# A hybrid encoder layer on one core: more attention rows turned by TensorE, turns a unit ahead, one more buffer for projection tiles

## The chip, the cores and the metric

The kernel runs on one core of a Trainium2 chip. The metric is the device time of one execution in microseconds (us); the median over runs is compared. Beside the runs there is one profiled execution, whose records make up the trace. TensorE (PE) multiplies matrices; VectorE (DVE), ScalarE (ACT) and GpSimd (POOL) work element by element; SyncE (SP) issues most DMA transfers. Each engine carries out its own instructions in order and waits for others by semaphores.

## The reference, cut to what matters

One encoder layer over 1024 tokens with 1024 features: a norm, one combined projection, two groups of attention heads beside each other, an output projection, and a gated MLP. The change lies in the attention.

```
proj = hn @ w_in;  qa, ka, va, qb, kb, vb = split(proj)
# group A: 8 query heads on 2 key heads, window |i - j| <= 128, a sink logit per head
p = softmax([q k / 8 within the window, sink]);  o_a = p v
# group B: 8 heads over a 16 x 64 grid of tokens, 8 x 16 neighbourhood, relative bias
p = softmax(q k / 8 + bias);                     o_b = p v
h = x + concat(rmsnorm(o_a), rmsnorm(o_b)) @ w_out
h = h + (silu(conv3(hn @ w_gate)) * (hn @ w_up)) @ w_down;  out = rmsnorm(h)
```

## The kernel before

**Splits.** All large products are made in three passes: a high and a low half of each operand, high by high, high by low and low by high (lines 156 to 158 for the projection). Every weight tile is loaded in two parts of 128x512 (`fetch_w`), copied to its high half by ScalarE (L148, `whi`), and its low half is a subtraction (L149, `wlo`) on DVE, or on POOL once the attention is well under way.

**Projection as filler.** The projection's columns are 18 jobs (`Project`), and then 8 jobs of the output projection for group A (`OutA`). Each job is 16 blocks of three matmuls of 128x512 into PSUM tiles `pj`; DVE moves a finished `pj` to a tile `t` of the pool "temps" (L224, L228), which has three buffers. The first three jobs are done ahead; the rest are spread as filler between the pieces of attention, by numbers per unit (`RATES`).

**Start.** Jobs 0 to 2 give the first key, value and queries of group A. Their rotation folds rows by DMA (`f<-t`), turns them on DVE (L242 to L244) and sends them back by DMA (`t<-f`, L246). Then come the stacks of high and low halves: keys (`split_first_k`, L271 to L274), queries (`split_first`, L264 and L265). The value tile is split to 16-bit halves `vhl`, a tile in "temps", and turned by a transposing DMA (L329, `v<-vhl`) that SyncE issues like the others. Loading of the second weight part of the third filler job is put behind the stacks.

**Attention.** There are 16 units of group A (a block of 128 queries, four heads each) and 32 of group B (a pair of query blocks, four units per head). A row is one query block of one head against up to three neighbouring key blocks. Its steps: TensorE makes the scores `s` (L378); DVE adds mask or bias, takes the extremum and writes `p` (L408); ScalarE exponentiates with the sum (L412); DVE takes the reciprocal (L413). Then the probabilities must be turned, keys to partitions, as two 16-bit halves in a tile `turned`, by one of three paths:

- D: ScalarE scales and copies the high half (L426), DVE makes the low half (L427), a transposing DMA turns both (L428).
- P: POOL scales (L416), ScalarE copies the high half (L422), POOL makes the low half (L423), a transposing DMA turns both.
- T: POOL scales (L416), TensorE transposes `p` block by block into the PSUM tile `pt` (L434), ScalarE copies the high half (L437), DVE makes the low half (L438).

Group A's four rows go by "DPTT", group B's eight rows of a head by "DPDPDPDP". TensorE then multiplies values by the turned rows into `o` (L461 in A, L534 in B), ScalarE and DVE take `o` out (L472 and L476; L548 and L550). Beside B, group A's result is squared and normed (L185, L187, L195, L218, L772), and POOL makes the bias tiles (L492, L493).

**Order.** TensorE's order is the program's, written out by the loop over units: in unit u the value products of u, the scores of a unit two or three ahead (`LEAD`), the turns of unit u itself (`T_AT`), and filler. The other engines and the DMA queues are ordered by a scheduler. Rings set what can run ahead: six tiles `p` (`PS`), four of `turned` (`TURNED`), with some rows of both groups in spare tiles of another pool (`SPARE_A`, `SPARE_B`: in B units 1 and 3 of heads 0 to 3, unit 3 of heads 4 and 5, none in heads 6 and 7), three staging tiles (`hl`, `stage`) for the DMA paths, two PSUM tiles each of `s`, `pt`, `o` and `pj`.

Of the kernel before, what the change touches and what calls it, by code (L numbers as in the profile page):

```python
# [34 lines left out]
FILL0, FILL1 = 22, 12  # L35
RATES = [41, 49, 22, 22, 22, 22, 20, 18, 16, 14]
AHEAD = 4
TURNED, PS, HLS, SPARE_A, LOWS = 4, 6, 1, (2, 5), 1
LEAD = 3
BIAS0 = 8  # L40
T_AT = (0, 4)
PATH_A, PATH_B = "DPTT", "DPDPDPDP"
SPARE_B = [(1, 3), (1, 3), (3,), ()]
WARM = 8

# [15 lines left out]
def hybrid_layer(tc, xT, w_in, w_out, w_gate, w_up, w_down, small, sink, rpb, consts, rope, out):  # L61
    nc = tc.nc
    with ExitStack() as ctx:
# [4 lines left out]
        attention_pools = ctx.enter_context(ExitStack())  # L68
        inner = lambda name, bufs: attention_pools.enter_context(tc.tile_pool(name=name, bufs=bufs))
        wpool = inner("weights", 3)  # L70
        tpool = inner("temps", 3)
        apool = inner("att", 2)
        spool = inner("stats", 6)
        vpool = inner("values", 4)
# [3 lines left out]
        def big(name, tag, dt=F32):  # L78
            return lpool.tile([128, S], dt, name=name, tag=tag, bufs=slots[tag])
# [7 lines left out]
        f32 = lambda ap: ap.bitcast(F32)  # L87
# [57 lines left out]
        def halve_w(raw):  # L145

            hi, lo = (wpool.tile([128, 4, 128], F32R, name=n, tag=n) for n in ("whi", "wlo"))
            mark["weights"] = nc.scalar.activation(hi, raw, AF.Copy)  # L148
            mark["weights low"] = (nc.gpsimd if LOWS and mark.get("attention") else nc.vector).tensor_tensor(lo, raw, f32(hi[:, :, :]), op=ALU.subtract)  # L149
            return [(hi[:, j, :], lo[:, j, :]) for j in range(4)]  # L150

        def load_w(src):
# [144 lines left out]
            nc.sync.dma_start(f32(a[o:o + 64, :]), f32(b[e:e + 64, :]))  # L297
            return a, b

        both = []  # L300
        gains, ups = cpool.tile([128, 8], F32, name="gains"), [None] * 8

        def scaled_gain(i, up, c):
# [3 lines left out]
        def split_v(t, rows):  # L307

            n = rows.stop - rows.start
            top, down = (vpool.tile([128, 1], F32, name=x, tag=x) for x in ("top", "down"))  # L310
            up = cpool.tile([128, 1], F32, name="up", tag="up", bufs=6)
            nc.vector.tensor_reduce(top[rows], t[rows, :], axis=mybir.AxisListType.X, op=ALU.max, apply_absolute_value=True)
            nc.vector.tensor_scalar(top[rows], top[rows], TINY, None, op0=ALU.max)
            nc.vector.tensor_scalar(top[rows].bitcast(I32), top[rows].bitcast(I32), 0x7F800000, None, op0=ALU.bitwise_and)
            nc.vector.reciprocal(down[rows], top[rows])
            nc.vector.tensor_scalar(down[rows], down[rows], V_TOP, None, op0=ALU.mult)
            nc.vector.tensor_scalar(up[rows], top[rows], 1.0 / (V_TOP * P_TOP), None, op0=ALU.mult)
            if n == 64:
                nc.gpsimd.tensor_copy(up[0:64], up[rows])
            flat = tpool.tile([128, 2 * S], F16, name="vhl", tag="t", padded_shape=[128, 2 * S + 4])  # L320
            hl = flat[:, :].rearrange("p (c s w) -> p c s w", s=2, w=128)
            if n == 128 or not both:
                both.append(big("v", "op").bitcast(F16)[:, :].rearrange("p (e c s w) -> p e c s w", c=NB, s=2, w=64))
            v = both[-1] if n == 128 else both[0][:, len(va):len(va) + 1]
            src = t[rows, :].rearrange("p (c w) -> p c w", w=128)
            mark["value"] = nc.scalar.activation(hl[rows, :, 0], src, AF.Copy, scale=down[rows])
            nc.vector.scalar_tensor_tensor(hl[rows, :, 1], src, down[rows], hl[rows, :, 0], op0=ALU.mult, op1=ALU.subtract)
            for i, k in enumerate(range(rows.start, rows.stop, 64)):
                nc.sync.dma_start(v[:, i].rearrange("p c s w -> p (c s) w"), flat[k:k + 64], transpose=True)  # L329
# [167 lines left out]

        def units_grid(h):

            st = {"begun": [False, False]}  # L500
            e = 64 * (h % 2)
            me, other = slice(e, e + 64), slice(64 - e, 128 - e)

            def q_step(b):
                def go():
                    if b == 0:
                        bias_of[h] = bias_of.pop(h, None) or bias_tiles(h)
                    if b == 4 and h < 7:
                        bias_of[h + 1] = bias_tiles(h + 1)
                    x = bias_of[h]  # L510
                    if b % 2 == 0:
                        st[b // 2] = Rows(b // 2 in SPARE_B[h // 2])
                    sel = slice(2, 5, 2) if b == 0 else slice(0, 3, 2) if b == NB - 1 else slice(1, 4)
                    ps, n = scores(qb[h], kb[h], b, True)
                    st[b // 2].softmax(PATH_B[b], b % 2, ps, n, x[:, sel, :], None, int(b == 0))
                return go

            def v_step(c):
                def go():
                    if c == 0:  # L520
                        st["o"] = [bank("o", "o") for _ in range(2)]
                    for half in range(2):
                        inb = [b for b in near(c) if b // 4 == half]
                        if not inb:
                            continue
                        final = c == (4 if half == 0 else NB - 1)
                        pairs = sorted({b // 2 for b in inb})
                        for k in pairs:
                            mine = [b for b in inb if b // 2 == k]
                            dst = st["o"][half][:, (mine[0] % 4) * 128:(mine[-1] % 4 + 1) * 128]  # L530
                            runs = st[k].tile[:, :, :, :, :].rearrange("p b i s q -> p (b i) s q")
                            k0 = 3 * (mine[0] % 2) + c - mine[0] + 1
                            for s in range(2):
                                nc.tensor.matmul(dst, vb[h][:, c], runs[:, k0:k0 + 2 * len(mine) - 1:2, s], start=not st["begun"][half],  # L534
                                                 stop=final and s == 1, skip_group_check=True)
                                st["begun"][half] = True
                        if final:
                            leave(half)
                return go

            def leave(half):
                i = 4 + h // 2
                if mix[i] is None:
                    mix[i] = big("mixb", "mix")
                ot = apool.tile([128, HALF], F32, name="ot", tag="ot", bufs=1)
                w = lambda ap: ap.rearrange("p (b r c) -> p b r c", r=ROWS, c=8)
                o = st["o"][half]
# [5 lines left out]
            return [([q_step(2 * i), q_step(2 * i + 1)], [v_step(c) for c in chunks[i]], []) for i in range(4)]  # L553


        done = set()
# [100 lines left out]
        t = quarters(big("f", "mix"))  # L657
# [13 lines left out]
        raw, hi, lo = big("raw3", "mix"), big("whi3", "mix", F32R), big("wlo3", "mix", F32R)  # L671
# [29 lines left out]
        with tc.high_priority(offset=400):  # L701
            with behind("turned"):
                turn(third.m, third.t)
            with behind("value"):
                nc.scalar.activation(warm, eps, AF.Exp)

        live = {"op": 0}
        needs = lambda m: 2 if m < 6 else 3 if m % 3 else 1
# [19 lines left out]
        def rest():  # L728
            for i, job in enumerate(jobs[1:]):
# [15 lines left out]
                        aux[i, n]()  # L745
                if i == 0:
                    with behind("stack", "copied"):
                        jobs[2].load_rest()
                    with behind("weights", "weights low"):
                        make_stacks(third)  # L750
                if isinstance(job, Project):
# [37 lines left out]
        for g in range(2):  # L789
            for b in range(NB):  # L790
                q, t, w = unit_window(g, b)
# [8 lines left out]
        flat = []  # L800
# [43 lines left out]
        for u in range(len(flat)):  # L844
            q, t, need, kind, _ = flat[u]
# [690 lines left out]
```

## Time and profile before

| | |
|---|---|
| median of 3 runs (lowest, highest) | 1095.08 us (1090.98, 1095.76) |
| profiled execution, its time | 1093.65 us |
| its span, first to last instruction | 1091.9 us |
| mean granted TensorE clock | 0.986 |
| busy, share of the span: PE, DVE | 96%, 79% |
| ACT, POOL | 51%, 17% |
| DMA packets under 512 bytes | 89408 of 150157 |

The span is 1.75 us shorter than the time of the same execution. Windows of the trace are in us from the span's start. In its rows a form such as `128x384 f16<-128x384 f32 x24 | 16.9, 705 | 3.7` gives shapes and count, the time in all and the mean of one in ns, and the idle time before them with what ended it. Matmuls overlap, so their own durations add up to more than the time that passes; how far apart they start tells what one costs.

### The profile page before, as it was taken

The numbers are of one execution on the slowest core, as the hardware profiler recorded it, in microseconds if no ns is written. First come the engines' busy times: TensorE is split into PE (matmuls) and PEld (weight loads), VectorE is DVE, ScalarE is ACT, GpSimd is POOL, SyncE is SP. The second block draws the span as 40 slices with busy tenths as digits, with TensorE's granted clock in tenths as the row PEclk, the third lists the DMA queues.
The fourth block names the chain that finished last, engine by engine and source line by source line (L and its number), as shares of the span: only waits on it lengthen the run. The fifth ranks groups of instructions, "written<-read, shape, count | busy, mean of one in ns | idle before, by whom it ended". The sixth has DMA issues, their size and how long they took to land.

```text
span 1091.9 us, 14925 instructions
## 1 busy us (share of the span) xinstructions
PE 1045.9 (96%) x4950; PEld 844.8 (77%) x4950; DVE 859.5 (79%) x1671; ACT 553.7 (51%) x1047; POOL 180.5 (17%) x263
## 2 busy tenths in 40 slices
PE   9988999999888899999999999999999999999997
PEld 7766677777666687787788888888888887888887
DVE  7688888766876588899988877877887857997764
ACT  7166777666666534545434334342433545554451
POOL 2324444455554300000000000000000000000001
PEclk9989999999999899999999999999999999999998
DMA  7335464798799736314333222322322788866644
GB/s 274 74 75 128 111 127 96 149 181 157 137 148 198 166 120 230 107 36 147 146 133 118 106 106 97 116 97 105 117 88 97 238 280 280 293 225 229 207 158 154
DMA packets 150157, 165.14 MB, mean 151 GB/s; under 512 B 89408, under 2 KB 100672, under 8 KB 150080
## 3 DMA queue, kind: packets, MB, share of 16 engines
q1 hardware_dynamic: 139424, 138.43, 46.3%
q10 hardware_dynamic: 10656, 25.76, 6.3%
q8 instruction: 39, 0.64, 0.2%
q14 instruction: 38, 0.31, 0.1%
HBM read 103.58 MB, written 28.57 MB: 121 GB/s over the span
## 4 chain that ended last, share of the span: by engine, by line
PE 53%; DVE 9%; DMA 5%; issue 1%; ACT 1%; POOL 0%; DVEq 0%; SPq 0%; ACTq 0%
PE dn L932 5%; PE dn L931 5%; PE dn L933 5%; PE z L933 4%; PE z L931 4%; PE z L932 4%; PE x L931 3%; PE x L932 3%; PE x L933 3%; PE y L933 3%; PE y L931 3%; PE y L932 3%; DMA raw<-in_w_down_dram 2%; DVE wlo L921 2%; PE pj L156 2%; PE pj L157 2%
## 5 line engine op out<-in xcount | busy, mean ns | idle before, releaser
L920 ACT ACTIVATE whi<-ws 128x512 fp32r<-128x512 f32 (+1 forms) x100 | 60.2, 623 | 129.1 <-DVE ws L1037 82.5
L932 PE MATMUL dn<-xd,whi 128*128 128x512 f32 (+1 forms) x330 | 123.9, 376 | 0.8 <-DVE xd L1250 0.8
L931 PE MATMUL dn<-xd,whi 128*128 128x512 f32 (+1 forms) x330 | 124.1, 376 | 0.0
L933 PE MATMUL dn<-xd,wlo 128*128 128x512 f32 (+1 forms) x330 | 123.8, 375 | 0.0
L156 PE MATMUL pj<-xgh,whi 128*128 128x512 f32 x248 | 108.3, 437 | 6.1 <-DVE t L228 3.4
L1357 POOL TENSOR_TENSOR h<-h,wide 128x256 f32<-128x256 f32 (+1 forms) x6 | 5.4, 926 | 626.6 <-ACT wide L1353 626.6
L933 PE MATMUL z<-hg,wlo 128*128 128x512 f32 x264 | 103.1, 390 | 0.6 <-DVE wlo L921 0.6
L931 PE MATMUL z<-hg,whi 128*128 128x512 f32 x264 | 102.8, 390 | 0.0
L932 PE MATMUL z<-hg,whi 128*128 128x512 f32 x264 | 102.7, 389 | 0.0
L158 PE MATMUL pj<-xgh,wlo 128*128 128x512 f32 x248 | 99.3, 400 | 1.6 <-DVE wlo L149 1.6
L157 PE MATMUL pj<-xgl,whi 128*128 128x512 f32 x248 | 98.8, 399 | 0.0
L412 ACT ACTIVATE p<-p,nm 128x385 f32<-128x385 f32 (+3 forms) x128 | 74.5, 583 | 35.7 <-DVE nm L408 28.2
L921 DVE TENSOR_TENSOR wlo<-ws,whi 128x512 fp32r<-128x512 f32 (+1 forms) x100 | 66.6, 680 | 18.1 <-ACT whi L920 18.0
L921 DVE TENSOR_TENSOR wlo<-raw,whi 128x512 fp32r<-128x512 f32 (+1 forms) x90 | 58.7, 672 | 21.8 <-ACT whi L920 19.4
L920 ACT ACTIVATE whi<-raw 128x512 fp32r<-128x512 f32 (+1 forms) x90 | 53.8, 615 | 38.1 <-DMA raw<-in_w_down_dram 15.1
L932 PEld LDWEIGHTS dn<-xd,whi 128*128 128x128 f32 x330 | 62.1, 188 | 12.6 <-DVE xd L1250 1.5
L1249 ACT ACTIVATE xd<-xd 128x512 fp32r<-128x512 f32 x77 | 47.0, 625 | 48.0 <-DMA xd<-x 47.8
L933 PEld LDWEIGHTS dn<-xd,wlo 128*128 128x128 f32 x330 | 62.1, 188 | 11.1
L931 PEld LDWEIGHTS dn<-xd,whi 128*128 128x128 f32 x330 | 62.1, 188 | 11.1
L933 PE MATMUL y<-hg,wlo 128*128 128x512 f32 x176 | 68.7, 390 | 1.4 <-DVE wlo L921 1.4
L1250 DVE TENSOR_TENSOR xd<-xd 128x512 fp32r<-128x512 f32 x77 | 51.9, 686 | 22.1 <-ACT xd L1249 21.6
L931 PE MATMUL x<-hg,whi 128*128 128x512 f32 x176 | 68.7, 390 | 0.0
(228 smaller groups left out, 2663.7 us busy)
## 6 DMA issues: line engine op xcount, KB each, us to landing
xd<-x SPq DMA_DIRECT2D x77, 256.0 KB, 4.7
raw<-in_w_down_dram SPq DMA_DIRECT2D x64, 256.0 KB, 4.1
raw<-in_w_gate_dram SPq DMA_DIRECT2D x22, 512.0 KB, 3.3
raw<-in_w_up_dram SPq DMA_DIRECT2D x22, 512.0 KB, 3.6
x<-c ACTq DMA_DIRECT2D x22, 512.0 KB, 2.9
raw<-in_w_in_dram SPq DMA_DIRECT2D x32, 256.0 KB, 3.0
raw<-in_w_down_dram SPq DMA_DIRECT2D x32, 192.0 KB, 4.4
x<-t ACTq DMA_DIRECT2D x11, 512.0 KB, 2.7
```

The costliest lines, as they stand in the source:

```text
L156: nc.tensor.matmul(ps, w[0], x[0][:, tsl(h)], start=first, stop=False)
L157: nc.tensor.matmul(ps, w[0], x[1][:, tsl(h)], start=False, stop=False)
L158: nc.tensor.matmul(ps, w[1], x[0][:, tsl(h)], start=False, stop=last)
L412: nc.scalar.activation(p[:, 0:e], p[:, 0:e], AF.Exp, bias=nm, scale=-1.0, accum_out=sm)
L920: nc.scalar.activation(hi, src, AF.Copy)
L921: nc.vector.tensor_tensor(lo, src, f32(hi[:, :, :]), op=ALU.subtract)
L931: nc.tensor.matmul(ps, w[0], x[0], start=first and i == 0, stop=False, skip_group_check=True)
L932: nc.tensor.matmul(ps, w[0], x[1], start=False, stop=False, skip_group_check=True)
L933: nc.tensor.matmul(ps, w[1], x[0], start=False, stop=last and i == len(ws) - 1, skip_group_check=True)
L1249: nc.scalar.activation(hi, f32(lo), AF.Copy)
L1250: nc.vector.tensor_tensor(lo, f32(lo), f32(hi), op=ALU.subtract)
L1357: nc.gpsimd.tensor_tensor(x, x, copy[:, cols], op=ALU.mult)
```

## The change

- `PATH_B` is now a list by head: "PPTPPPTP" for heads 0 and 1, "TPTPTPTP" for heads 2 to 7. No row of B goes by D. Where before 32 rows of B went by D and 32 by P, there are now 36 by P and 28 by T.
- The turns are no longer made in their own unit. In unit u stand the turns of unit u + 1, at places 3 and 8 among the events of group A's units (`T_NEXT`), at 0 and 3 for group B (`T_B`); only unit 0 keeps its own.
- The rings: "temps" gets a fourth buffer, `turned` goes from 4 to 3, `p` from 6 to 5.
- Before the filler begins, `vhl` lies in a tile of the pool of operands ("op") instead of "temps", and the first transposing DMA of values is held back and issued behind the last rotated rows of jobs 0 to 2 (the mark "back").
- POOL instead of DVE makes the low half of one early weight part (the mark "early").

```diff
-TURNED, PS, HLS, SPARE_A, LOWS = 4, 6, 1, (2, 5), 1
+TURNED, PS, HLS, SPARE_A, LOWS = 3, 5, 1, (2, 5), 1
-PATH_A, PATH_B = "DPTT", "DPDPDPDP"
+PATH_A, PATH_B = "DPTT", ["PPTPPPTP"] * 2 + ["TPTPTPTP"] * 6
+T_B, T_NEXT = (0, 3), (3,8)
...
-        tpool = inner("temps", 3)
+        tpool = inner("temps", 4)
...
-            mark["weights low"] = (nc.gpsimd if LOWS and mark.get("attention") else nc.vector).tensor_tensor(lo, raw, f32(hi[:, :, :]), op=ALU.subtract)
+            mark["weights low"] = (nc.gpsimd if mark.get("attention") or mark.get("early") else nc.vector).tensor_tensor(lo, raw, f32(hi[:, :, :]), op=ALU.subtract)
...
-            flat = tpool.tile([128, 2 * S], F16, name="vhl", tag="t", padded_shape=[128, 2 * S + 4])
+            if mark.get("begun"):
+                flat = tpool.tile([128, 2 * S], F16, name="vhl", tag="t", padded_shape=[128, 2 * S + 4])
+            else:
+                flat = big("vhl", "op").bitcast(F16)
...
+            if mark.get("begun"):
+                across()
+            else:
+                postponed.append(across)
...
-                    st[b // 2].softmax(PATH_B[b], b % 2, ps, n, x[:, sel, :], None, int(b == 0))
+                    turn[b] = st[b // 2].softmax(PATH_B[h][b], b % 2, ps, n, x[:, sel, :], None, int(b == 0))
...
+            later = lambda b: lambda: turn[b]()
+            return [([q_step(2 * i), q_step(2 * i + 1)], [v_step(c) for c in chunks[i]], [later(b) for b in (2 * i, 2 * i + 1) if PATH_B[h][b] == "T"]) for i in range(4)]
...
+            with behind("back"):
+                postponed.pop()()
+        mark["begun"] = True
...
                     with behind("stack", "copied"):
+                        mark["early"] = True
                         jobs[2].load_rest()
+                        mark["early"] = False
...
-            for i, w in enumerate(flat[u][4]):
-                events.insert(T_AT[i], ("v", w))
+            if u == 0:
+                for i, w in enumerate(flat[u][4]):
+                    events.insert(T_AT[i], ("v", w))
+            if u + 1 < len(flat):
+                for i, w in enumerate(flat[u + 1][4]):
+                    events.insert((T_NEXT if u < 15 else T_B)[i], ("v", w))
```

What moves is shown at three places by the order of the built programs, where line numbers of the changed one are up to 20 higher.

SyncE's queue at the start, before: `f<-t` folds rows, `t<-f` and `t<-turns` send rotated rows back, `v<-vhl` turns the first values.

```order
L240 DMA f<-t 128x1x128 x2
L240 DMA turns<-t 128x1x128
L329 DMA_TRANSPOSE v<-vhl 128x16x64
L246 DMA t<-f 16x8x128 x4
L246 DMA t<-turns 16x8x128 x2
```

The same place now:

```order
L241 DMA f<-t 128x1x128 x2
L241 DMA turns<-t 128x1x128
L247 DMA t<-f 16x8x128 x4
L247 DMA t<-turns 16x8x128 x2
L334 DMA_TRANSPOSE v<-vhl 128x16x64
```

The transposing DMA went from before the six rows that go back to behind them.

TensorE in a unit of head 4 of group B, before: scores, filler, then values by turned rows.

```order
L378 MATMUL s<-ka,q 128x256
L378 MATMUL s<-kb,q 128x256
L156 MATMUL pj<-xgh,whi 128x512
L157 MATMUL pj<-xgl,whi 128x512
L158 MATMUL pj<-xgh,wlo 128x512
L534 LDWEIGHTS v
```

The same scores now:

```order
L388 MATMUL s<-ka,q 128x256
L388 MATMUL s<-kb,q 128x256
L157 MATMUL pj<-xgh,whi 128x512
L158 MATMUL pj<-xgl,whi 128x512
L159 MATMUL pj<-xgh,wlo 128x512
L444 MATMUL pt<-cst,p 128x128 x3
```

A turn of three blocks, for the unit after, now stands at the head of the unit, ahead of its value products.

POOL on the first rows of group B, before: L416 scales a row, L423 makes its low half, L149 is a weight's low half.

```order
L423 TENSOR_TENSOR hl<-p,hl 128x3x128
L416 TENSOR_SCALAR p<-p,sm 128x384
L423 TENSOR_TENSOR stage<-p,stage 128x3x128
L149 TENSOR_TENSOR wlo<-raw,whi 128x512
L416 TENSOR_SCALAR p<-p,sm 128x384
L423 TENSOR_TENSOR stage<-p,stage 128x3x128
L149 TENSOR_TENSOR wlo<-raw,whi 128x512
L492 TENSOR_TENSOR xb<-cst,rr 128x384
```

The same place now, from the low half of the first full row on to the bias tile of head 1:

```order
L433 TENSOR_TENSOR hl<-p,hl 128x3x128
L426 TENSOR_SCALAR p<-p,sm 128x384
L433 TENSOR_TENSOR stage<-p,stage 128x3x128
L426 TENSOR_SCALAR p<-p,sm 128x384
L150 TENSOR_TENSOR wlo<-raw,whi 128x512
L433 TENSOR_TENSOR stage<-p,stage 128x3x128
L426 TENSOR_SCALAR p<-p,sm 128x384
L433 TENSOR_TENSOR hl<-p,hl 128x3x128
L150 TENSOR_TENSOR wlo<-raw,whi 128x512
L502 TENSOR_TENSOR xb<-cst,rr 128x384
```

One more row with both halves stands on POOL between the same weight tiles and the same bias tile.

More of the change, by code (lines that the diff above doesn't have):

```diff
@@ L298, in split_k @@
             return a, b
-        both = []
+        both, postponed = [], []
         gains, ups = cpool.tile([128, 8], F32, name="gains"), [None] * 8
@@ L327, in split_v, with across @@
             nc.vector.scalar_tensor_tensor(hl[rows, :, 1], src, down[rows], hl[rows, :, 0], op0=ALU.mult, op1=ALU.subtract)
-            for i, k in enumerate(range(rows.start, rows.stop, 64)):
-                nc.sync.dma_start(v[:, i].rearrange("p c s w -> p (c s) w"), flat[k:k + 64], transpose=True)
+            def across():
+                for i, k in enumerate(range(rows.start, rows.stop, 64)):
+                    nc.sync.dma_start(v[:, i].rearrange("p c s w -> p (c s) w"), flat[k:k + 64], transpose=True)
+            if mark.get("begun"):
+                across()
+            else:
+                postponed.append(across)
             return [v[:, i].rearrange("p c s w -> p c (s w)") for i in range(n // 64)], up
@@ L498, in units_grid @@
         def units_grid(h):
-            st = {"begun": [False, False]}
+            st, turn = {"begun": [False, False]}, {}
             e = 64 * (h % 2)
@@ L552, in units_grid @@
             chunks = [[0], [1, 2], [3, 4], [5, 6, 7]]
-            return [([q_step(2 * i), q_step(2 * i + 1)], [v_step(c) for c in chunks[i]], []) for i in range(4)]
+            later = lambda b: lambda: turn[b]()
+            return [([q_step(2 * i), q_step(2 * i + 1)], [v_step(c) for c in chunks[i]], [later(b) for b in (2 * i, 2 * i + 1) if PATH_B[h][b] == "T"]) for i in range(4)]
         done = set()
```

## The prediction

> **What bounds the kernel now.** The windows view was read first, over the stretches around the attention phase. Its columns are the busy time of TensorE (PE), its weight loads, VectorE (DVE), ScalarE (ACT) and GpSimd (POOL), then the granted TensorE clock, the DMA share and GB/s.
>
> ```profile
> 65.00:206.00 141.00, 130.84 (x718) 98.94 (x716) 121.89 (x402) 102.25 (x261) 63.41 (x133) 0.99 0.53 112
> 206.00:273.00 67.00, 66.67 (x356) 52.24 (x356) 43.26 (x132) 43.81 (x103) 35.83 (x40) 1.00 0.90 171
> 273.00:312.00 39.00, 31.15 (x166) 24.24 (x165) 33.91 (x84) 24.53 (x55) 23.70 (x25) 0.95 0.73 132
> 312.00:380.00 68.00, 61.54 (x309) 46.58 (x308) 42.42 (x116) 41.37 (x91) 29.96 (x33) 0.90 0.89 175
> ```
>
> TensorE is the bound everywhere, with holes: at the start (before 65, below), through group A (65 to 206) and from 273 on in group B; from 206 to 273 there is none, so that anything added to TensorE there is paid in full. The holes by what ended them, from TensorE's waits in 55 to 195 and in 195 to 410 (total, times, longest):
>
> ```profile
> PE o L461 <- DVE mixa L476: 3.6, 2, 1.9
> PE o L461 <- ACT turned L437: 3.1, 4, 1.1
> PE pj L156 <- ACT whi L148: 2.7, 1, 2.7
> PE o L461 <- DVE turned L438: 1.6, 6, 0.4
> PE pj L158 <- DVE wlo L149: 1.6, 1, 1.6
> ...
> PE st L195 <- DVE sq L187: 4.0, 1, 4.0
> PE o L534 <- DMA turned<-stage: 3.5, 2, 2.9
> PE pj L156 <- DVE t L228: 3.4, 1, 3.4
> PE o L534 <- DMA turned<-hl: 2.5, 1, 2.5
> ```
>
> Together 26.0 us. A long hole costs more than itself: TensorE's timeline has one that ends at 359.96,
>
> ```profile
> 359.96 0.37 PE L534 MATMUL o<-turned,v 128*128 128x128 f16 x2 [2.90 <-DMA turned<-stage]
> ```
>
> and for six us behind it the clock is granted at half. The windows view over the stretch behind each long hole gives that clock, and length times (1 - clock) is the time lost:
>
> ```profile
> 60.50:68.00 7.50, 5.72 (x16) 4.41 (x17) 5.79 (x9) 3.90 (x8) 0.00 (x0) 0.62 0.19 52
> ...
> 277.80:282.00 4.20, 3.66 (x13) 2.92 (x14) 4.17 (x10) 2.33 (x6) 2.87 (x3) 0.65 0.37 83
> 309.80:314.00 4.20, 4.09 (x16) 3.16 (x17) 4.11 (x10) 2.93 (x6) 2.06 (x2) 0.70 1.22 145
> 339.00:342.50 3.50, 3.37 (x12) 2.66 (x12) 1.67 (x5) 2.38 (x6) 2.86 (x4) 0.55 1.00 187
> 359.90:366.00 6.10, 6.04 (x19) 4.78 (x19) 2.28 (x7) 3.86 (x9) 3.68 (x4) 0.50 0.67 168
> ```
>
> That is (the start first) 2.85, 1.47, 1.26, 1.58 and 3.05 us, 10.2 in all. So waits and slow clock are worth some 36 us, and the change must pay for its transposes out of them.
>
> **Part 1, the start.** The timeline of all queues before the first scores (SPq is SyncE's DMA queue):
>
> ```profile
> 50.12 2.74 SPq L329 DMA_TRANSPOSE v<-vhl  x1
> 52.96 2.50 SPq L246 DMA_DIRECT2D t<-f  x4
> 54.17 0.69 DVE L224 TENSOR_TENSOR t<-pj,rstd 128x512 f32<-128x512 f32 x1 [1.83 <-DMA v<-vhl]
> ...
> 55.71 1.06 ACT L271 ACTIVATE ka<-t 64x1024 fp32r<-64x1024 f32 x1 [7.58 <-DMA t<-f]
> ...
> 60.04 0.63 ACT L148 ACTIVATE whi<-raw 128x512 fp32r<-128x512 f32 x1
> ...
> 62.28 0.68 DVE L149 TENSOR_TENSOR wlo<-raw,whi 128x512 fp32r<-128x512 f32 x1
> ```
>
> The value transpose stands ahead of the rotated rows on SyncE's queue; those release ka, the stacks, and behind them whi (60.04), for which TensorE has waited 2.7 us. Moved behind the rows, it lets them go 2.8 us earlier. L224, which waited for the same transpose to give its projection buffer back, is freed too: vhl sits in another pool and there is a fourth buffer. Then whi ends at about 57.9, and the 2.7 us go. The low half, on POOL at 1.3 us a time (row below) instead of queued on DVE until 62.28, ends near 59.2; TensorE wanted it at 62.96 - 1.6 = 61.4, 0.7 us behind whi, now at about 58.7, so 0.5 of the 1.6 us stays. Without a long hole the 2.85 us of slow clock go as well: 2.7 + 1.1 + 2.85 = 6.7. But the second query stack on the same chain also moves by only 2.8, and the third score row needs it. Bounds 2.8 and 7.1; I take **-5**, nearer the upper end, since two of the three waits are on this chain alone. The value transpose itself is not missed: TensorE's first product with values stands behind two units of scores.
>
> **Part 2, turns a unit ahead in group A.** The 3.1 + 1.6 = 4.7 us that value products waited for fresh turns go. In their place the turn itself can wait for POOL: it now stands some 10 of 14 events behind its scores, and 141 us for 16 units make that about 6 us; the way from scores to scaled row took, for one row,
>
> ```profile
> 101.20 0.34 PE L378 MATMUL s<-ka,q 128*128 128x384 f32 x1
> ...
> 105.75 0.71 POOL L416 TENSOR_SCALAR p<-p,sm 128x384 f32<-128x384 f32 x1
> ```
>
> 5.3 us. So there is hardly any cover: bounds are nothing given back and all 4.7; I take 2.2, that is **-2.5**. The 3.6 us on mixa (L476) stay, since no edit touches them. The smaller p ring (5) costs nothing as long as rows of A are held one unit instead of two; without that cover a score waits on DVE.
>
> **Part 3, the added transposes.** 28 rows of B turn on TensorE, 78 blocks of 128 (the first block of a head has two neighbours, not three). Price from group A's rows:
>
> ```profile
> 89.88 0.49 PE L434 MATMUL pt<-cst,p 128*128 128x128 f32 x3
> 90.12 0.47 PE L156 MATMUL pj<-xgh,whi 128*128 128x512 f32 x1
> 90.44 0.39 PE L157 MATMUL pj<-xgl,whi 128*128 128x512 f32 x1
> 90.67 0.40 PE L158 MATMUL pj<-xgh,wlo 128*128 128x512 f32 x1
> ...
> L434 PE MATMUL pt<-cst,p 128*128 128x128 f32 x88 | 14.8, 272 | 0.4 <-POOL p L416 0.4
> ```
>
> Three take 0.24 us of the sequence (89.88 to 90.12), and the projection matmul behind them 0.32 (to 90.44) instead of the 0.23 of the next (to 90.67). Per row 0.24 to 0.33, in all 6.7 to 9.2; I take **+7.5**, as some turns stand where TensorE changes operands anyway.
>
> **Part 4, DVE's waits in B** (4.0 on sq and 3.4 on t, with 1.47 + 1.26 of slow clock: 10.1). Means of one:
>
> ```profile
> L427 DVE SCALAR_TENSOR_TENSOR stage<-p,sm,stage 128x384 f16<-128x384 f32 x24 | 16.9, 705 | 3.7 <-ACT stage L426 2.0 <-issue 1.1 <-POOL wlo L149 0.4
> L438 DVE TENSOR_TENSOR turned<-pt,turned 128x384 f16<-128x384 f32 x24 | 13.2, 553 | 1.3 <-ACT turned L437 0.8
> ```
>
> A row with DVE's low half costs DVE 0.71 us and a small scaling, a turned one 0.55, a POOL row neither. Heads 0 and 1 lose eight of the first kind for four turned: 3.4 us less; heads 2 to 7 swap 24: 3.6 less. Seven us over eight heads, while TensorE gets 7.5 more to cover DVE; two holes of 3 to 4 us should shrink but not both vanish, as the squares of group A still crowd that place. Bounds 0 and 10.1; I take half: **-5**.
>
> **Part 5, DMA waits in B** (3.5 + 2.5, with 1.58 + 3.05: 10.6). 28 of B's 64 transposes through DMA are gone, where the DMA share stands at 0.90 and 0.89. ScalarE is freed as well, by the 12.6 us of this row of its groups (206 to 375):
>
> ```profile
> L422 ACT ACTIVATE stage<-p 128x384 f16<-128x384 f32 (+1 forms) x20 | 9.9, 497 | 28.0 <-POOL p L416 15.4 <-DMA turned<-stage 12.6
> ```
>
> Bounds 0 and 10.6; I take three quarters, **-8**, since the load that they share falls by almost half. The Trainium skill, "TensorE: Matmul & The Clock Gate", HAM oscillation, has the clock halve only after idle gaps of about 3.4 us; the trace shows it halved, or nearly, behind 2.9 and 2.5 us, and the measurement decides. By that rule of the Trainium skill the slow clock would not belong to these two waits, and this term would be -4.5.
>
> **Sum.** -5 - 2.5 + 7.5 - 5 - 8 = -13.0 against the profiled execution's 1093.65 (span 1091.9) gives 1080.6. The median of the runs, 1095.08, lies 1.4 above that execution, so the forecast is **1082**. Best ends of all terms: -7.1 - 4.7 + 6.7 - 10.1 - 10.6 = -25.8, or 1069.
>
> **Rivals.** (a) *POOL becomes the pace of B.* Its groups, first in 193 to 236, then in 236 to 370, and two means:
>
> ```profile
> L416 POOL TENSOR_SCALAR p<-p,sm 128x384 f32<-128x384 f32 (+1 forms) x10 | 5.8, 582 | 9.9 <-DVE sm L413 5.2 <-PE pj L158 4.7
> ...
> L416 POOL TENSOR_SCALAR p<-p,sm 128x384 f32<-128x384 f32 (+1 forms) x23 | 16.0, 694 | 33.5 <-DVE sm L413 33.3
> ...
> L423 POOL TENSOR_TENSOR stage<-p,stage 128x384 f16<-128x384 f32 x24 | 23.7, 986 | 18.5 <-ACT stage L422 18.3
> L149 POOL TENSOR_TENSOR wlo<-raw,whi 128x512 fp32r<-128x512 f32 x23 | 30.5, 1325 | 19.4 <-ACT whi L148 18.8 <-DMA turned<-hl 0.5
> ```
>
> Heads 0 and 1 bring four more rows with both halves there (0.58 + 0.99, and 18.5/24 of waiting in the middle: 9.4) and four scalings (2.3): 11.7 us into 9.9 of slack. ScalarE's copies queue behind POOL (15.4 above), DVE behind ScalarE. Then parts 4 and 5 give nothing, heads 0 and 1 run 2 late, and two new holes cost what the one at 339 does (2.5 + 1.6 each): -5 - 2.5 + 7.5 + 2 + 8.2 = +10, or **1105**. It decides once POOL has no idle time left there. Against it: scores run three units ahead, and heads 2 to 7 need only 24 x 0.69 = 17 of 33.5.
> (b) *Three "turned" slots instead of four.* In heads 6 and 7, which have no spare rows, a DMA row must wait for TensorE to leave the unit after the one that held its slot, and SyncE's queue with it. Two or three holes like that at 339 give 10 back: **1092**, no change. Against it: half the rows are now written a unit later, by TensorE.
> (c) *The transposes cost their full mean*, 78 x 0.272 = 21.2 instead of 7.5: **1096**, no change. Against it: the starts in part 3. The Trainium skill, "TensorE: Matmul & The Clock Gate", PE-mode transpose, gives some 275 ns for one in a kernel; the mean here agrees, the spacing of the starts does not.
> (d) *Nearly all ends well*: **1069**, if DVE and DMA both stop being late.
>
> **How the numbers follow.** Forecast (1073 to 1089) 0.50, (d) 0.17, (a) 0.15, (b) 0.12, (c) 0.06. Half a per cent (5.5 us) is about what a measurement of this kernel tells from no change. Faster takes the forecast, (d) and a quarter of (b): 0.70; within it (c) and the rest of (b): 0.15; slower (a): 0.15. The range cuts half of (d) and most of (a): 1068 to 1098; the forecast's own is 1073 to 1089.
>
> **What would show it.** In the profile after: no wait of pj on whi near 58 and a clock near 1.0 there; turns in A waiting on POOL p for 1 to 3 us in total; no row of value products waiting on turned from ACT or DVE; DMA share in B at 0.6 to 0.7; clock at 0.97 or more from 312 to 380. Wrong if L416's successor on POOL shows next to no idle time in heads 0 and 1 and TensorE waits on pt from POOL or on wlo, or if the value products of the last two heads still wait on DMA for 5 us.

## The result, and the profile after

| | before | after |
|---|---|---|
| median of 4 runs (lowest, highest) | 1094.61 us (1090.98, 1095.76) | 1076.11 us (1075.51, 1076.55) |
| ratio, 95% interval | | 0.9836 [0.9812, 0.986] |
| profiled execution, its time | 1093.65 us | 1075.93 us |
| its span | 1091.9 us | 1074.1 us |
| mean granted TensorE clock | 0.986 | 0.996 |
| DMA packets under 512 bytes | 89408 of 150157 | 68544 of 129293 |

The changed kernel is faster by 18.5 us in the medians and by 17.7 in the profiled executions. Where the time went is read from four views, each against its counterpart of before, which the prediction shows.

**Waits of TensorE.** First in 55 to 206 (the end of the start and group A), then in 206 to 410 (group B but for its first 20 us, and what lies behind it); total, times, longest:

```profile
PE o L471 <- DVE mixa L486: 2.9, 3, 2.0
PE pt L444 <- DVE turned L448: 2.8, 2, 1.5
PE pt L444 <- POOL p L426: 1.9, 3, 0.9
PE pj L159 <- POOL wlo L150: 1.4, 1, 1.4
PE o L471 <- ACT turned L447: 0.8, 1, 0.8
PE pj L157 <- ACT whi L149: 0.6, 1, 0.6
```

```profile
PE st L196 <- DVE nm L418: 1.7, 1, 1.7
PE pj L157 <- DVE t L229: 1.3, 1, 1.3
PE pt L444 <- DVE sm L423: 0.7, 1, 0.7
```

With their smaller rows these two lists add up to 10.6 and 4.5 us; before, the same windows had 14.3 and 14.6. In group A most of the holes have only changed their name: value products wait 0.8 instead of 4.7 us for fresh turns, and turns wait 1.9 us for POOL's scaled row and 2.8 us for a `pt` bank that DVE has not yet left. In group B they are gone: no row of value products waits on a transfer any more, and none of the holes that are left is longer than 1.7 us.

**The clock.** The windows view of after, with the prediction's columns; the second row is of a window within the first:

```profile
55.00:65.00 10.00, 8.02 (x29) 6.03 (x28) 9.46 (x12) 7.31 (x11) 2.02 (x1) 0.83 0.35 74
60.80:65.00 4.20, 4.20 (x13) 3.50 (x14) 3.77 (x7) 1.63 (x5) 0.00 (x0) 0.59 0.31 94
...
206.00:273.00 67.00, 65.27 (x361) 51.13 (x360) 41.51 (x121) 44.11 (x105) 42.95 (x54) 1.00 0.68 141
273.00:312.00 39.00, 37.56 (x214) 29.17 (x213) 31.53 (x78) 25.31 (x55) 25.02 (x32) 1.00 0.62 131
312.00:380.00 68.00, 67.27 (x377) 52.59 (x377) 48.47 (x115) 38.60 (x89) 35.12 (x42) 1.00 0.55 136
```

In 312 to 380 TensorE is busy for 67.27 instead of 61.54 us, at full clock instead of 0.90, and the DMA share has fallen from 0.89 to 0.55. Of the five stretches of slow clock only the one at the start is left, with 4.2 x (1 - 0.59) = 1.7 us of the 10.2.

**The start.** The timeline of all queues:

```profile
50.28 3.15 SPq L247 DMA_DIRECT2D t<-f  x4
...
53.69 1.06 ACT L272 ACTIVATE ka<-t 64x1024 fp32r<-64x1024 f32 x1 [5.40 <-DMA t<-f]
...
54.76 1.36 SPq L334 DMA_TRANSPOSE v<-vhl  x1
...
57.15 2.46 DVE L266 SCALAR_TENSOR_TENSOR q<-t,q 64x1024 fp32r<-64x1024 f32 x2
...
58.02 0.63 ACT L149 ACTIVATE whi<-raw 128x512 fp32r<-128x512 f32 x1
...
58.73 2.02 POOL L150 TENSOR_TENSOR wlo<-raw,whi 128x512 fp32r<-128x512 f32 x1 [11.57 <-ACT whi L149]
...
60.80 0.57 PE L159 MATMUL pj<-xgh,wlo 128*128 128x512 f32 x1 [1.36 <-POOL wlo L150]
```

The value transpose now leaves behind the rotated rows, which go 2.7 us earlier (50.28 against 52.96). They take longer, 3.15 instead of 2.50 us for the first four, so that `ka` and `whi` are only 2.0 us earlier each.

**ScalarE and POOL in group B.** Groups of instructions, first of 206 to 360, then of POOL in 187 to 230 and in 230 to 355 (count, time in all, mean, and the idle time before them):

```profile
L432 ACT ACTIVATE stage<-p 128x384 f16<-128x384 f32 (+1 forms) x21 | 10.2, 487 | 23.9 <-POOL p L426 23.9
...
L426 POOL TENSOR_SCALAR p<-p,sm 128x384 f32<-128x384 f32 (+1 forms) x18 | 10.0, 555 | 4.2 <-DVE sm L423 3.0 <-DVE up L318 1.1
...
L426 POOL TENSOR_SCALAR p<-p,sm 128x384 f32<-128x384 f32 (+1 forms) x46 | 27.4, 596 | 27.0 <-DVE sm L423 18.9 <-PE pt L444 2.4 <-DVE top L315 2.2
```

ScalarE's 12.6 us of waiting for a staging tile that a transfer still held are gone. POOL has less slack in heads 0 and 1, but has some: 4.2 us before the scalings, and 27.0 in the heads behind.

**Where it was gained**, from the moment of the k-th row of scores in both timelines (after minus before): first row -2.4 us, row 8 -4.2, row 64 (the first of group B) -5.5, row 112 -8.7, last row -16.6; the last value product of B -15.9, the end of the span -17.7. So the start gave 4.2, the rest of group A 1.3, group B 10.4 and what lies behind the attention 1.8 us.

### The profile page after: what moved, and what is told of

Its sections match the earlier page's. It is cut to its first block, busy times and chain, and to the rows that moved or that the text cites. A ratio compares the mean times of both kernels' runs of the same rounds, so it can differ in the third digit from the quotient of the medians.

```text
span 1074.1 us, 15094 instructions
## 1 busy us (share of the span) xinstructions
PE 1045.2 (97%) x5028; PEld 847.6 (79%) x5028; DVE 849.8 (79%) x1634; ACT 549.9 (51%) x1047; POOL 197.1 (18%) x300
## 2 busy tenths in 40 slices
DMA packets 129293, 160.02 MB, mean 149 GB/s; under 512 B 68544, under 2 KB 79808, under 8 KB 129216
## 4 chain that ended last, share of the span: by engine, by line
PE 74%; DVE 13%; DMA 3%; POOL 3%; ACT 3%; issue 3%; SPq 0%; DVEq 0%; POOLq 0%; ACTq 0%
PE dn L951 7%; PE dn L952 7%; PE dn L953 7%; PE pj L157 5%; PE pj L159 5%; PE pj L158 5%; PE z L953 5%; PE z L952 4%; PE z L951 4%; PE x L952 3%; PE x L951 3%; PE x L953 3%; PE y L953 3%; PE y L952 3%; PE y L951 3%
## 5 line engine op out<-in xcount | busy, mean ns | idle before, releaser
L426 POOL TENSOR_SCALAR p<-p,sm 128x384 f32<-128x384 f32 (+1 forms) x112 | 66.7, 598 | 50.5 <-DVE sm L423 38.9
```

The source lines that it names most:

```text
L426: nc.gpsimd.tensor_scalar(x, x, sm, P_TOP, op0=ALU.mult, op1=ALU.mult)
```

## The experiments

Differences "to after" are those of medians; each ratio is to before, with its 95% interval. Where two kernels are close, that comparison is over different chips, and differences under about 1 us are not read.

**The start alone.** The kernel before with the diff's edits on `vhl`, "back" and "early" and nothing else; then the reverse, the kernel after without these. The cut shows the main lines.

```diff
 # the start alone: before, with
+            if mark.get("begun"): ... else: flat = big("vhl", "op").bitcast(F16)
+                postponed.append(across)
+            with behind("back"):
+                postponed.pop()()
+                        mark["early"] = True
```

> The kernel before with the edits of the start alone: value halves in a tile of the operands' pool, first value transpose behind the rotated rows, one low weight half on POOL. Theory: these alone bring the first scores of group A about 4 us forward and nothing later gives it back, so 4 to 5 us less than before (about 1090). Rival: group A is paced by VectorE, which is busy 86% there, and swallows what the start gains: less than 1.5 us. The waits on DMA and VectorE in group B stay as before under both.

> The changed kernel without the edits of the start: paths, turns ahead and rings alone. Theory (parts add): 13 to 14 us less than before (about 1081), 4 to 5 more than the changed kernel. Rival (the start was swallowed): the same as the changed kernel, 17 to 18 less than before.

The start alone: 1087.82 us, 0.9943 [0.9929, 0.9956], 6 us under before. Without the start: 1079.66, 0.9872 [0.9857, 0.9887], 14 us under before. The two parts are nearly independent (6 + 14 against 18.5). The first profile keeps the holes of group B nearly as they were; its waits in 206 to 410 begin so:

```profile
PE st L195 <- DVE sq L187: 4.3, 1, 4.3
PE o L543 <- DMA turned<-stage: 3.5, 3, 2.8
PE pj L156 <- DVE t L228: 3.0, 1, 3.0
PE o L543 <- DMA turned<-hl: 2.5, 1, 2.5
```

**The rows of B back on the old paths.** The kernel after with group B's old pattern; start, rings and turns a unit ahead stay.

```diff
-PATH_A, PATH_B = "DPTT", ["PPTPPPTP"] * 2 + ["TPTPTPTP"] * 6
+PATH_A, PATH_B = "DPTT", ["DPDPDPDP"] * 8
```

> The changed kernel with the old paths DPDPDPDP in all heads of group B; start, turns ahead in group A and rings stay changed. Theory (the gain beyond the start and group A is that of the turned rows): the kernel with the start alone less 2 to 3 us, that is 8 to 9 less than before (about 1085) and 9 more than the changed kernel, with the holes on sq, t and turned from DMA back and a slow clock behind them. Rival (the rings and the fourth buffer did it): within 2 us of the changed kernel.

1086.25 us, 0.9931 [0.9915, 0.9947]: 10.1 us slower than after. TensorE's waits in 206 to 410 (the longest in total), and the windows view behind its longest holes:

```profile
PE pj L157 <- ACT whi L149: 4.0, 1, 4.0
PE o L544 <- DMA turned<-stage: 3.3, 6, 1.7
PE pj L157 <- DVE t L229: 2.9, 1, 2.9
PE o L544 <- DMA turned<-hl: 2.5, 1, 2.5
```

```profile
270.00:274.00 4.00, 2.70 (x7) 1.78 (x8) 2.97 (x8) 3.21 (x7) 4.00 (x4) 0.50 0.43 92
274.00:278.00 4.00, 4.00 (x20) 3.00 (x19) 3.58 (x8) 1.33 (x5) 3.88 (x4) 0.69 0.88 202
306.10:310.50 4.40, 4.39 (x16) 3.35 (x16) 4.28 (x9) 2.87 (x5) 1.96 (x2) 0.62 1.12 145
334.40:338.60 4.20, 4.20 (x16) 3.24 (x16) 2.94 (x8) 3.45 (x8) 2.20 (x2) 0.59 0.95 144
359.80:364.00 4.20, 4.19 (x23) 3.44 (x24) 3.45 (x11) 2.25 (x7) 1.38 (x2) 1.00 0.62 102
```

The windows are those behind the holes of 4.0 us (ended at 270.05, two windows), 2.9 (306.11), 2.5 (334.40) and 1.7 (359.81, on `stage`). With D rows the holes on transfers return and so does the one on DVE's `t`. The longest hole, on `sq` before, now stands on `whi` from ScalarE; on DVE's `sq`, where it was expected, there is none. The slow clock is back behind the three longest: 2.0 + 1.2 + 1.7 + 1.7 = 6.6 us of it. The waits of the whole list are 14.3 us where after has 4.5. So the views hold 9.8 + 6.6 = 16.4 us that the rows on TensorE save. Less some 8.6 for their transposes (below) that leaves 7.8. From the first row of scores of B to its last value product this profile is 8.4 us longer than after's; 1.1 us more lie ahead of B, where this execution has a slow clock at 126 us that after's has not, and 0.9 behind it. The smaller rings, which this kernel keeps, are no large part of it: the kernel with the start alone has the old rows and the old rings, and takes 1087.8 against 1086.3.

**Which load of the D rows it was.** Two kernels give back one load each. One sends the two halves of 28 of the 36 P rows a second time through the transposing DMA, into a scratch tile (in the kernel with three "temps" buffers, which makes room for that tile); the other makes the low half of every T row in B twice on DVE.

```diff
 # DMA load back: after, with temps 3
+                    if nsink is None and next(extra):
+                        nc.sync.dma_start(scratch[:, 0:c].rearrange(...), hl[:, 0:c], transpose=True)
 # DVE load back: after
+                    for _ in range(times):    # 2 in group B
                         nc.vector.tensor_tensor(lo, apart(ps[:, 0:c * 128]), hi, op=ALU.subtract)
```

> The kernel with three projection buffers, and 28 of the DMA rows of group B send their halves a second time, to a scratch tile, so that as many transposes go through DMA in group B as before, while VectorE keeps its relief. Theory 1 (the gain of group B is the load taken off DMA): 7 to 11 us more than the kernel with three buffers, with waits of value products on DMA and a clock near 0.9 from 312 to 380 again. Theory 2 (it is VectorE's relief): 0 to 2 us more, no such waits.

> The changed kernel with the low half of each turned row of group B made twice on VectorE (28 times 0.55 = 15 us more there, twice what the change took off it). Theory (half of VectorE's waits in group B, some 5 us, went because it was relieved): 4 to 8 us more than the changed kernel, with holes of TensorE on VectorE between 260 and 312. Rival (VectorE was late only because ScalarE ahead of it waited for DMA): 0 to 1.5 us more.

> The changed kernel with three buffers for projection tiles instead of four. Theory (the fourth buffer was only cover, the value tile of the start no longer competes for it): 0 to 2 us more than the changed kernel. Rival (the buffer removes the waits of TensorE on t): 4 us more or beyond, with a hole of 3 us on t and a slow clock behind it.

Three buffers alone: 1077.68 us, 0.9853 [0.9838, 0.9868]. With the transfers: 1083.74, 0.991 [0.9897, 0.9924], so the 28 pairs of transfers cost 6.1. With DVE's extra 15 us: 1078.96, 0.986 [0.9842, 0.9878], 2.9 us to after, though these two intervals overlap; the change relieved DVE by about half of that load. The windows of the DMA kernel and then of the DVE kernel, 206 to 380:

```profile
206.00:273.00 67.00, 65.88 (x364) 51.52 (x361) 42.85 (x120) 43.65 (x102) 42.45 (x54) 1.00 0.88 171
273.00:312.00 39.00, 36.95 (x211) 28.76 (x211) 30.86 (x78) 25.45 (x56) 24.88 (x31) 1.00 0.82 152
312.00:380.00 68.00, 63.52 (x355) 48.56 (x354) 43.69 (x110) 37.44 (x87) 35.38 (x43) 1.00 0.71 171
```

```profile
206.00:273.00 67.00, 66.83 (x368) 52.17 (x367) 47.09 (x131) 44.33 (x105) 44.02 (x55) 1.00 0.67 143
273.00:312.00 39.00, 35.64 (x201) 27.57 (x202) 32.79 (x80) 23.35 (x52) 24.49 (x30) 1.00 0.66 126
312.00:380.00 68.00, 65.99 (x368) 50.50 (x367) 52.08 (x124) 39.06 (x89) 36.47 (x42) 1.00 0.55 138
```

The DMA load weighs more than DVE's, but neither alone brings back, in its profile, a hole that slows the clock: in the first the longest wait in 206 to 410 is 2.1 us (a `pt` on DVE's `sm`), and the waits of value products on transfers that were expected are a single one of 0.9; in the second the longest is 1.6 us (a `pj` on DVE's `t`). The first profile is of the fastest of five runs (1081.05 us, granted clock 0.998); the other four took 2.5 to 3.2 us more at 0.994 to 0.997, so that slow clock can be a part of the 6.1. The losses expected, 7 to 11 for DMA and 4 to 8 for DVE, were both too high, and those of their rivals too low. No run gives both loads back at once.

**The price of the transposes.** Each transpose of B twice into the same place of its bank.

```diff
-                for i in range(c):
+                for i in list(range(c)) * times:    # 2 in group B
```

> The changed kernel with the transposes of the turned rows of group B made twice on TensorE (78 blocks more). Theory (TensorE is the bound in group B, and three blocks cost 0.24 us of its sequence): 5.5 to 7.5 us more than the changed kernel. Rival c of the prediction (each costs its full mean of 0.27 us): 21 us more. A second rival (TensorE has room for them): less than 2 us more.

1080.63 us, 0.9881 [0.9866, 0.9896]: 4.5 us to after for 78 more blocks, a little under the 5.5 to 7.5 expected. TensorE's timeline, of after and then with each block doubled:

```profile
220.95 0.49 PE L444 MATMUL pt<-cst,p 128*128 128x128 f32 x3
221.19 0.47 PE L157 MATMUL pj<-xgh,whi 128*128 128x512 f32 x1
221.51 0.39 PE L158 MATMUL pj<-xgl,whi 128*128 128x512 f32 x1
```

```profile
220.13 0.81 PE L444 MATMUL pt<-cst,p 128*128 128x128 f32 x6
220.70 0.47 PE L157 MATMUL pj<-xgh,whi 128*128 128x512 f32 x1
```

Three blocks take 0.24 us of the sequence (and the projection matmul behind them 0.09 more than the 0.23 of one in a stream), six take 0.57. In place the second three cost 0.33 us a row, 0.11 a block, or 78 x 0.11 = 8.6 us. The time grew by 4.5 only. TensorE's waits in group B (187 to 353) fell from 3.7 to 0.7 us: work added to TensorE is partly work that it would have waited through. For the two profiles the sum closes: 8.6 - 3.0 = 5.6, less the 1.7 us of slow clock at the start that after's has and this one has not, is the 3.9 between their times. Before and after agree with the price: from the first row of scores of B to its last value product TensorE was busy for 171.11 us before, 7.36 of them lost to slow clock, and for 171.87 after, which makes 8.1 us more of work.

**The turns back in their own unit**, in A and B, with the rest of the change.

```diff
-            if u == 0:
-                for i, w in enumerate(flat[u][4]):
-                    events.insert(T_AT[i], ("v", w))
-            if u + 1 < len(flat):
-                for i, w in enumerate(flat[u + 1][4]):
-                    events.insert((T_NEXT if u < 15 else T_B)[i], ("v", w))
+            for i, w in enumerate(flat[u][4]):
+                events.insert(T_AT[i], ("v", w))
```

> The changed kernel with each turn in its own unit again, at the old places. Theory (turns a unit ahead gave 1 to 2 us in group A, and in group B they keep the copies of ScalarE and VectorE off TensorE's path, 0.5 to 1 us for each of 28 rows where they stand right before their products): 8 to 20 us more than the changed kernel, with waits of value products on turned from ScalarE and VectorE. Rival (the place does not matter, the rings cover it): less than 2 us more.

1098.47 us, 1.0044 [1.0029, 1.0058]: 22 us to after, slightly more than expected, and slower than before. TensorE's waits in 206 to 410 (the longest in total), and its busy time in B:

```profile
PE o L544 <- DVE turned L448: 8.0, 21, 1.0
PE o L544 <- ACT turned L447: 6.5, 10, 1.7
```

```profile
206.00:380.00 174.00, 158.38 (x866) 120.85 (x865) 109.88 (x288) 104.10 (x238) 98.13 (x124) 1.00 0.62 132
```

The value products stand and wait 31 times for 28 T rows, 0.4 and 0.7 us each on average, and in this profile (1095.73 us, clock 0.997) the clock stays at 1.00; the slower of the ten runs have it at 0.990 to 0.996. Of the 19.8 us between the profiles some 2.4 lie in group A (rows of scores 8 to 64) and nearly all the rest in B. There the waits account for some 13: from the first row of scores to the last value product TensorE stands idle for 16.6 us instead of 3.9. Some 6 more are in a longer busy time (178.2 us instead of 171.9) for the same work, which was not taken apart. So T rows in B pay only because their turns stand a unit ahead: with old rows the kernel takes 1086, with T rows in their own unit 1098, with T rows a unit ahead 1076.

**All rows of B on P**, to see whether POOL could have become the pace.

```diff
+PATH_A, PATH_B = "DPTT", ["PPPPPPPP"] * 8
```

> The changed kernel with all rows of group B on path P: VectorE relieved even more, DMA as loaded as before, no transposes of group B on TensorE, and 64 rows with both halves on POOL. Theory (POOL can carry some 9 rows per 20 us with their wait in the middle, and the turned rows are what spares both POOL and DMA): POOL becomes the pace, 10 us more than the changed kernel or beyond. Rival (relief of VectorE is what counts, POOL has slack): within 3 us of the changed kernel.

1089.06 us, 0.9957 [0.9942, 0.9972]: 13 us to after. The windows, and the groups of 206 to 375:

```profile
206.00:273.00 67.00, 60.56 (x315) 46.58 (x314) 35.65 (x100) 40.63 (x98) 50.54 (x62) 0.98 0.82 158
```

```profile
L426 POOL TENSOR_SCALAR p<-p,sm 128x384 f32<-128x384 f32 (+1 forms) x58 | 38.2, 659 | 12.5 <-DVE sm L423 12.0
L432 ACT ACTIVATE stage<-p 128x384 f16<-128x384 f32 (+1 forms) x39 | 19.2, 494 | 37.9 <-POOL p L426 32.7 <-DMA turned<-stage 5.1
```

DVE is at 35.65 of 67 us here, lower than in any other kernel of the study, and the time is still 13 us worse: ScalarE waits 32.7 us for POOL in the row shown, and TensorE 6.7 for transfers and 6.5 for DVE's `t` in two holes, with four stretches of slow clock (0.95 over 206 to 380). That POOL is the pace is not shown by this: it is busy for 127 of 174 us in 206 to 380, and all 64 rows go through DMA again, which alone cost 6.1 above.

**Where T rows pay most, and a last version.** Old rows in the first three heads, then in the first two; then the latter with group A's turns at places 5 and 10.

```diff
+PATH_A, PATH_B = "DPTT", ["DPDPDPDP"] * 3 + ["TPTPTPTP"] * 5
 # or
+PATH_A, PATH_B = "DPTT", ["DPDPDPDP"] * 2 + ["TPTPTPTP"] * 6
 # and then
-T_B, T_NEXT = (0, 3), (3,8)
+T_B, T_NEXT = (0, 3), (5, 10)
```

> The changed kernel with the old paths DPDPDPDP in heads 0 to 2 of group B and turned rows from head 3 on. Theory (where TensorE had no hole before, from 206 to 273, a turn is paid in full): 8 turned rows fewer at 0.27 us, 2 us less than the changed kernel. Rival (what heads 0 to 2 add to VectorE and DMA comes out as holes between 270 and 312): 3 us more or beyond.

> The changed kernel with the old paths in heads 0 and 1 alone, turned rows from head 2 on. Theory (no hole stood in heads 0 and 1, and head 2 needs its turned rows against the hole on sq near 272): 4 turned rows less at 0.27 us and no new hole, 1 us less than the changed kernel. Rival (what heads 0 and 1 put on VectorE and DMA is still late at 272): 0 to 3 us more.

> The kernel after, with DPDPDPDP in heads 0 and 1 (as in the run with two old heads, 1075.2 us) and group A's turns at places 5 and 10 instead of 3 and 8. Theory 1: at 3 and 8 the turns stand too close behind POOL and DVE (1.9 us on POOL p, 2.8 us on a pt bank that DVE has not left); later they find both ready, and the value products of the next unit still come late enough: these 4.7 us fall to 1 or 2, and the time to 1071 to 1074. Rival: the turned tiles come late for the value products again (before the change 4.7 us of waits on ACT and DVE), the waits only change sides: 1074 to 1078, with waits of o on turned of 2 to 5 us in 65 to 206.

Three old heads: 1075.25 us, 0.983 [0.9816, 0.9845]; what is gained up to row 88 is lost in a new hole of 2.1 us where scores wait for DVE's `turned`. Two old heads: 1075.22, 0.9832 [0.9814, 0.9851]. Neither can be told from after. With the later turns too: 1072.76, 0.982 [0.9798, 0.9843], the lowest median of the study, 3.4 us under after, though the intervals overlap. TensorE's longest waits in 65 to 206 of this last kernel:

```profile
PE o L471 <- DVE mixa L486: 4.4, 4, 1.7
PE pt L444 <- DVE turned L448: 2.3, 3, 1.7
```

The wait on POOL's `p` is gone, that on the `pt` bank has shrunk little, and value products wait 1.5 us more on `mixa` instead. Between rows 8 and 64 of the scores this gained 2.2 us over the kernel with two old heads. The time lies in the range of theory 1 (1071 to 1074) and below the rival's; the 4.7 us of waits fell to 2.3 and not to 1 or 2, and the waits on `turned` that the rival named did not come.

## Why the prediction was right

The forecast was 1082 us, the result 1076.11, faster and within the range; the likeliest case held, and it came out better than its sum by 4.7 us (-17.7 against -13.0 on the profiled execution).

- **Part 1, the start (-5).** Right in kind and size: 6 us alone, 4.2 by row 8 in after's profile. Two steps of it failed. The rows that go back took longer, so `whi` came 2.0 us earlier and not 2.8, and 0.6 us of TensorE's wait on it stayed. POOL's low half took 2.02 us instead of 1.3 (58.73), so the wait on it was 1.36 us and not the 0.5 named, and behind it this execution has the clock at 0.59 for 4.2 us, where 1.0 was named as the sign. The fourth buffer was counted only inside this part; taken out alone it costs some 1.6 us, little more than such a comparison can tell.
- **Part 2, turns ahead in A (-2.5).** About right: the profiles give 1.3 between rows 8 and 64, the turns back in their own unit lose 2.4 there. Of the waits on fresh turns one of 0.8 us stayed, where none was named as the sign. The waits on POOL that were to come back as 2.2 us are 1.9; not foreseen were the 2.8 us on the `pt` bank.
- **Part 3, the transposes (+7.5).** The price was right: 0.33 us a row of three with the matmul behind it, some 8.6 in all (8.1 by the busy time of B), between the bounds of 6.7 and 9.2. Rival (c), 21.2 us, is refuted by the doubling.
- **Parts 4 and 5, the waits of B (-5 and -8).** Here lies the error. The net of parts 3 to 5 was to be -5.5; group B gave 10.4 by its rows, 4.9 more. What lies behind the attention, in no part of the prediction, gave another 1.8. Against these stand 0.8 that the start and 1.2 that group A gave less than forecast, which makes the 4.7; that errors of both signs partly cancel is luck. With 8.1 to 8.6 for the transposes, the waits and their slow clock are worth some 19 us, or some 17 by the 8.4 us that the old rows lose in B, of the 20.7 named as the bound, and not 13. The fractions, a half and three quarters, were too low. DVE's share, tested alone, is small (2.9 us for twice the load), the transfers' is 6.1, and neither alone brings a long hole and a slow clock back in its profile. Why D rows cost more than these two loads, some 17 to 19 against 6.1 and at most 2.9, was not taken apart further; that the two loads together cost more than their sum is untested. That a D row ties ScalarE, DVE and a staging tile to the end of a transfer, in program order, is a possible link, but it is only argued.
- **The clock behind the waits of B** was counted with them, and rightly: it fell behind holes of 2.5 and 2.9 us in before (0.55 and 0.50) and again in the run with old rows (0.59 and 0.62), and not where these holes are gone. The rule of the Trainium skill, "TensorE: Matmul & The Clock Gate", HAM oscillation, that gaps above some 3.4 us are needed, is not borne out by these four holes.
- **The rivals.** (a) did not come: the slack in heads 0 and 1 went from 9.9 us to 4.2, and not to nothing. With 64 rows on POOL instead of 36 the time is 1089 us, but that run loads DMA again too, so it does not show POOL as the pace. (b) is refuted: no value products wait on transfers in B with three slots. (d), 1069, was too much to hope for: the 10.6 us of waits in group A stayed.
- **What was not priced at all**: turns a unit ahead in group B. They were taken as given with the T rows; without them the change is slower than before.

Against the trace as a whole: TensorE's waits fell by 3.7 us in 55 to 206, by 10.1 in 206 to 410 and by 3.1 outside (10.6 to 7.5), the slow clock by 8.5; the transposes cost 8.6. That makes -16.8 of the -17.7 measured. The 3.1 of waits outside attention were in no part of the prediction.

## What to carry to other kernels

Moving work onto the engine that is the bound can pay, if that work is a small part of what the bound engine now waits for, and if its producers and consumers are given a whole unit of distance; put beside its consumer, the same work cost more than it saved. Price the added work by the spacing of starts, and expect less than that where holes are left to fill. Count waits and the clock behind them as one term: of the 13 holes of some 2.5 us and more that TensorE has in group B in the profiles of before, the start alone, old rows and all rows on P, 12 were followed by a slow clock, which cost 1.3 to 3.2 us each in the two profiles worked out above.

## What the runs showed of the hardware

- **Whether short waits slow the clock changes from one execution to the next.** The same two waits, 0.5 to 0.7 and 1.36 us with 0.74 us of work between them, stand near 58 to 62 us in all twelve profiles that have the new start. Behind them the clock is slow in four (after, the start alone, DVE's load, old rows) and 1.00 in the other eight. The wait of 2.0 us on `mixa` at 124 to 130 us, in ten profiles, is followed by a slow clock in three (without the start, three old heads, old rows). Even a hole of 3.0 us on `t` was followed by a clock of 1.00, once, in the run with the start alone (305.7). After's row is above; with doubled transposes it reads:

```profile
60.80:65.00 4.20, 4.20 (x21) 3.40 (x22) 4.14 (x8) 1.62 (x5) 0.00 (x0) 1.00 0.30 94
```

  The Trainium skill, "TensorE: Matmul & The Clock Gate", What's actually happening, has activity judged in a free-running window of about 3.4 us, so that the place of a gap in it varies; that would fit two outcomes of one sequence. Its condition of an idle window does not fit, since TensorE stood idle for some 2 of 2.7 us here.
- **POOL's subtraction beside DVE.** The same 128x512 low half took 2.02 us at 58.73, where DVE was in the second of two SCALAR_TENSOR_TENSOR until 59.61. The 23 of before, from 183 us on, took 1.26 to 1.31 us but for two. Those two (1.71 us at 268.00 and 1.73 at 304.76), and two of after (1.76 at 266.25 and 2.35 at 311.67), also began while DVE was in an instruction that reads two tiles of SBUF, with 0.55, 0.58, 0.61 and 1.19 us of it left. Each time the subtraction took longer by that rest less some 0.14 us (0.89 left and 0.73 longer at 58.73); where such an instruction began after it, it took its usual time. The Trainium skill, "SBUF — State Buffer", SBUF: two separate sides, has DVE and GpSimd exclude each other on a shared pair of ports while an instruction with two such inputs runs, the one that starts first holding it to its end; which agrees.
